# Moving a mixer's element work off GpSimd, and regrouping its small matmuls, in a two-layer RWKV trunk kernel

## The chip, the cores and the metric

The kernel runs on one core of one Trainium2 chip. The metric is device time of the whole program, in microseconds. TensorE (PE) multiplies, VectorE (DVE), ScalarE (ACT) and GpSimd (POOL) do element work, and SyncE (SP) issues most of the weight DMAs.

## The reference

Two layers of a decoder trunk run over 256 prompt tokens and 32 sample tokens (8 sequences of 4), all with the same weights. Each layer is a half-step FFN, a mixer, and a second half-step FFN:

```python
u = _modnorm(x, norm_g[l, 0], mod[:, :, 0], mod[:, :, 1])
x = x + 0.5 * mod[:, :, 2] * _swiglu(u, w_ffn_in[l, 0], w_ffn_out[l, 0])
u = _modnorm(x, norm_g[l, 1], mod[:, :, 3], mod[:, :, 4])
p = u @ w_in[l]
ya, S_T, sh = _rwkv7(p[..., :A_PROJ], ...)
yb, ph = _pool(p[..., A_PROJ:], pool_in[l], pos, w_pool[l], pool_scale[l])
gates = sigmoid(u @ w_gate[l] + b_gate[l])
merged = gates[..., :D_MODEL] * (ya @ w_br_a[l]) + gates[..., D_MODEL:] * (yb @ w_br_b[l])
x = x + mod[:, :, 5] * (merged @ w_out[l])
# then the second FFN like the first
```

The branch `_rwkv7` mixes each projected row with the row of the token before (`xs = pa + (prev - pa) * mu`), forms r, k, v, a decay, a and a gate g, runs a recurrence over tokens on a 64x64 state for each of 8 heads, normalises the result per head, adds a bonus (the sum of r*k*r_k times v) and multiplies by g. The branch `_pool` takes running means over 2, 4, 8 and 16 tokens for four groups of 128 channels. D_MODEL is 1024, A_WIDTH and B_WIDTH are 512.

## The kernel before, in words

Activations lie channel-major: 128 channels on the partitions, NT = 288 tokens along the free axis. The big products run in fp32r with a correction: each strip of four 128x128 weight tiles comes by DMA (`raw`), ACT rounds it to `wh` (L224), DVE forms the remainder `wl` (L225), and `mm3` issues three matmuls for a tile (L250), chained in one fixed order on PE. Four strips can be split ahead. All other matmuls are ordinary fp32.

A layer's mixer first projects u by the 19 tiles of w_in and the gates ("ga") by eight tiles for each branch. The list MAIN says in which order these strips come. A generator runs through MAIN; the recurrence's small work is written as code that calls `fill()` between its pieces, and each `fill()` runs a planned number of strips or queued items. A queued item is followed by two strips (WEAVE = 2). So every small piece of PE work stands between strips of big matmuls, and a pool strip's result is used by `pool_out` one "ga" strip after it.

Preparation makes four sets of 64-column blocks: A, B (`bb`), K and R, from xk, xr, aa (the in-context rate), ep and en (running decays). AR holds A and R, BK holds B and K. `scores(e, i, q)` multiplies four 64-row blocks of one row half e into one PSUM bank (L892), and DVE masks it out of PSUM into MM (L894). Four banks (`pswk`) serve these and all other small products. From MM a 15-step triangular inverse runs on DVE (L933 to L936), and its merges go back to PE (L1158, L1167). Then a loop over four chunks of 64 tokens carries the state (L1255, L1268). While it runs, the bonus of each pair of heads is spread by a matmul (L806) and the gate is made (L1113, L1114), each as a queued item of its own; `outputs`, group norms and the sample group's pieces follow in the same queue.

GpSimd takes in the mixer: the sample columns' three operations of a norm's end (L488, L489, L492), part of the token shift (L659), the copies and window sums of the pools (L668, L675, L686, L687), most products of the preparation (L834 to L880), r*k for the bonus (L958), and R times the decay (L968). Names used below: `psmm` and `pswk` are PSUM banks, `dd` is the pool branch's input to its matmul (L693), `rkk` is r*k, `xn`, `uh`, `ul` are a norm's result and its two parts.

Of the kernel before, what the change touches and what calls it, by code (L numbers as in the profile page):

```python
# [21 lines left out]
ALU = mybir.AluOpType  # L22
# [165 lines left out]
class Kernel:  # L188
# [281 lines left out]
    def u(self, l, sub, k0=0, k1=KD):  # L470

        nc = self.nc
        e3 = nc.gpsimd if l + sub else nc.vector
# [135 lines left out]
    def mixer(self, l):  # L609
# [39 lines left out]
        def shifted(i, ps, dst, early=False):  # L649

            mu = self.par(l, "mu", i)
            S.activation(out=dst, in_=ps[:, :NT], func=AF.Copy, scale=mu1[:, i:i + 1])
            S.copy(sho[:, i, :], ps[:, TP - 1:NT:TS])
            V.scalar_tensor_tensor(out=dst[:, 1:TP], in0=ps[:, 0:TP - 1], scalar=mu, in1=dst[:, 1:TP],
                                   op0=ALU.mult, op1=ALU.add)
            d3, p3 = self.smp(dst[:, TP:]), self.smp(ps[:, TP:NT])
            V.scalar_tensor_tensor(out=d3[:, :, 1:], in0=p3[:, :, 0:TS - 1], scalar=mu, in1=d3[:, :, 1:],
                                   op0=ALU.mult, op1=ALU.add)
            (V if early else G).tensor_tensor(out=d3[:, :, 0], in0=d3[:, :, 0], in1=shs[:, i, :], op=ALU.add)  # L659

        def pooled(g, ps):
# [6 lines left out]
            G.tensor_copy(pxs[:, :, 0:HIST], po[:, 1:, :])  # L668
# [17 lines left out]
            G.tensor_copy(po[:, 0, :], px[:, TP:TP + HIST])  # L686
            G.tensor_copy(po[:, 1:, :], pxs[:, :, TS:])  # L687
# [26 lines left out]
        def project_pre(m, ps):  # L714
            p = p0[:, m % KD, :]
            c = self.scaled(ps, p, V if m < 5 else G)
# [13 lines left out]
        def main_ops():  # L730

            for n, (name, m) in enumerate(MAIN):
# [101 lines left out]
        G.tensor_copy(gam[:, :, 0:NCH], ep[:, :, CH - 1:TP:CH])  # L834
        G.tensor_copy(gam[:, :, NCH:], ep[:, :, TP + TS - 1:NT:TS])
# [16 lines left out]

        for j in range(HP):
            S.activation(out=A[:, j], in_=chunks(xk[:, j, :]), func=AF.Copy, scale=self.par(l, "k_k", j))
        k_k = self.par(l, "k_k").unsqueeze(2)
        G.tensor_tensor(out=ARs[:, :, 0, :], in0=xk[:, :, TP:], in1=k_k.to_broadcast([P, HP, NS]), op=ALU.mult)
        G.tensor_tensor(out=bb[:, :, TP:], in0=ARs[:, :, 0, :], in1=aa[:, :, TP:], op=ALU.mult)
# [14 lines left out]
        for j in range(HP):  # L872
# [4 lines left out]
            with tc.issue_after(b_en.ins):  # L877
                G.tensor_tensor(out=R[:, j], in0=chunks(xr[:, j, :]), in1=chunks(ep[:, j, :]), op=ALU.mult)
        G.tensor_tensor(out=BKs[:, :, 1, :], in0=xk[:, :, TP:], in1=en[:, :, TP:], op=ALU.mult)
        G.tensor_tensor(out=ARs[:, :, 1, :], in0=xr[:, :, TP:], in1=ep[:, :, TP:], op=ALU.mult)  # L880
# [7 lines left out]
        def scores(e, i, q):  # L888
            ps = self.ps_wk()
            r = halves[e]  # L890
            for hp in range(HP):
                T.matmul(ps[:, 128 * hp:128 * hp + 128], BK[r, hp, i, 2 * q:2 * q + 2, :].rearrange("p x t -> p (x t)"),  # L892
                         AR[r, hp, 2 * i + q].rearrange("p x t -> p (x t)"), start=True, stop=True)
            V.tensor_tensor(out=MM[:, 2 * e + i, :, q].rearrange("p h x t -> p h (x t)"),  # L894
                            in0=ps.rearrange("p (h y) -> p h y", h=HP), in1=maskp, op=ALU.mult)
# [15 lines left out]
        for i in range(2):  # L911
            for q in range(2):
                for e in range(2):
                    scores(e, i, q)
# [40 lines left out]
        def rkk(j):  # L955

            t = tj("rkk")
            G.tensor_tensor(out=t, in0=xr[:, j, :], in1=xk[:, j, :], op=ALU.mult)  # L958
            return t

        def bonus():
# [5 lines left out]
            for c in range(1, NCH):  # L967
                G.tensor_tensor(out=R[:, :, c], in0=R[:, :, c], in1=gam[:, :, c - 1:c].to_broadcast([P, HP, CH]),  # L968
                                op=ALU.mult)
# [134 lines left out]
        def out_gate(j):  # L1104

            if j == 0:
# [378 lines left out]
```

## Time and profile before

| what | value |
|---|---|
| runs | 1456.34, 1459.24 and 1464.87 us, median 1459.24 |
| the profiled execution's own time | 1455.73 us |
| its span | 1453.9 us |
| PE / DVE / ACT / POOL busy | 1408.2 / 938.7 / 724.7 / 200.4 us |
| the two mixers | about 264 to 500 us and 978 to 1213 us |

PE is busy nearly all the time, so the profile is read from PE's idle gaps and from its small matmuls, then from the engine that ended each gap. The second mixer repeats the first some 713.7 us later with the same waits, so most rows are shown of the first alone. A row of a timeline gives the start, the duration and the instruction; consecutive starts on PE are what a matmul costs, since its recorded durations overlap.

### The profile page before, as it was taken

How to read it: one execution, taken by the hardware profiler on the slowest of the kernel's cores; microseconds unless marked ns; L12 is line 12 of the kernel's file. 1: busy time of each engine (PE TensorE's matmuls, PEld its weight loads, DVE VectorE, ACT ScalarE, POOL GpSimd, SP SyncE). 2: the span in 40 equal slices, each digit the busy share in tenths (PEclk: the TensorE clock that was granted, in tenths of full speed). 3: DMA queues.
4: the chain of work that ended last, by engine and by line, in shares of the span. 5: the costliest groups of instructions: out<-in, count | busy, mean ns of one | idle time of the engine just before them, and what ended most of it. 6: DMA issues, size and time to landing. Idle time of an engine off the chain costs nothing.

```text
span 1453.9 us, 30079 instructions
## 1 busy us (share of the span) xinstructions
PE 1408.2 (97%) x11872; PEld 1301.8 (90%) x11872; DVE 938.7 (65%) x1996; ACT 724.7 (50%) x1457; POOL 200.4 (14%) x294
## 2 busy tenths in 40 slices
PE   6999999998999999999999999999989999999997
PEld 5989999987778999899999999998877799999997
DVE  4645556898656885555667555669966678755554
ACT  4544444674534665444445445448553356645532
POOL 0000011163113010000211000122522110100012
PEclk9999999999999999999999999999999999999999
DMA  8888764443324666787657644553333257445552
GB/s 358 315 280 308 301 241 146 150 131 107 100 77 162 254 248 229 273 305 268 244 215 257 238 155 163 167 169 120 111 93 119 99 176 274 160 146 167 167 163 103
DMA packets 72382, 281.93 MB, mean 194 GB/s; under 512 B 9584, under 2 KB 11504, under 8 KB 62896
## 3 DMA queue, kind: packets, MB, share of 16 engines
q1 hardware_dynamic: 66384, 272.24, 53.0%
q10 hardware_dynamic: 5856, 7.77, 1.7%
q8 instruction: 93, 1.52, 0.4%
q14 instruction: 49, 0.40, 0.1%
HBM read 275.74 MB, written 4.23 MB: 193 GB/s over the span
## 4 chain that ended last, share of the span: by engine, by line
PE 85%; DVE 9%; issue 2%; ACT 1%; POOL 1%; DMA 1%; POOLq 0%; DVEq 0%; ACTq 0%
PE psmm L250 43%; PE pswk L250 30%; PE psmd L314 4%; DVE wl L225 3%; DVE ul L483 1%; DVE xn L480 1%; PE pswk L1134 1%; PE pswk L392 1%; PE pswk L902 0%; PE pswk L1036 0%; DVE g L936 0%; DMA s<-in_wkv 0%; PE pswk L1255 0%; DVE sh L933 0%; DMA cc<-in_c 0%
## 5 line engine op out<-in xcount | busy, mean ns | idle before, releaser
L225 DVE TENSOR_TENSOR wl<-raw,wh 128x512 fp32r<-128x512 f32 x732 | 522.2, 716 | 365.6 <-ACT wh L224 357.2
L224 ACT CAST wh<-raw 128x512 fp32r<-128x512 f32 x732 | 452.5, 620 | 564.8 <-PE psmm L250 296.2
L250 PE MATMUL psmm<-uh,wh 128*128 128x288 f32 x1072 | 324.2, 302 | 2.3 <-ACT uh L491 2.3
L250 PE MATMUL psmm<-uh,wl 128*128 128x288 f32 x1072 | 318.1, 297 | 4.0 <-DVE wl L225 4.0
L250 PE MATMUL psmm<-ul,wh 128*128 128x288 f32 x1072 | 318.1, 297 | 0.6 <-DVE ul L492 0.3
L250 PEld LDWEIGHTS psmm<-uh,wh 128*128 128x128 f32 x1072 | 202.6, 189 | 23.3 <-issue 11.9
L250 PEld LDWEIGHTS psmm<-uh,wl 128*128 128x128 f32 x1072 | 202.6, 189 | 8.1 <-DVE wl L225 5.2
L250 PEld LDWEIGHTS psmm<-ul,wh 128*128 128x128 f32 x1072 | 202.7, 189 | 3.1 <-issue 1.2
L250 PE MATMUL pswk<-ul,wh 128*128 128x288 f32 x608 | 179.6, 295 | 0.0
L250 PE MATMUL pswk<-uh,wl 128*128 128x288 f32 x608 | 179.5, 295 | 0.0
L250 PE MATMUL pswk<-uh,wh 128*128 128x288 f32 x608 | 179.5, 295 | 0.0
L377 POOL TENSOR_TENSOR sq<-x 128x288 f32<-128x288 f32 x28 | 19.8, 706 | 770.6 <-DVE x L519 770.6
L250 PEld LDWEIGHTS pswk<-uh,wh 128*128 128x128 f32 x608 | 114.6, 188 | 5.4 <-issue 4.2
L250 PEld LDWEIGHTS pswk<-ul,wh 128*128 128x128 f32 x608 | 114.6, 188 | 0.0
L250 PEld LDWEIGHTS pswk<-uh,wl 128*128 128x128 f32 x608 | 114.5, 188 | 0.0
L250 PE MATMUL pswk<-hl,wh 128*128 128x288 f32 x352 | 103.8, 295 | 0.0
L250 PE MATMUL psmm<-hl,wh 128*128 128x288 f32 x352 | 103.8, 295 | 0.0
L250 PE MATMUL psmm<-hh,wl 128*128 128x288 f32 x352 | 103.8, 295 | 0.0
L250 PE MATMUL pswk<-hh,wl 128*128 128x288 f32 x352 | 103.7, 295 | 0.0
L250 PE MATMUL psmm<-hh,wh 128*128 128x288 f32 x352 | 103.7, 295 | 0.0
L250 PE MATMUL pswk<-hh,wh 128*128 128x288 f32 x352 | 103.2, 293 | 0.0
L314 PE MATMUL psmd<-modw,csilu 128*32 128x512 f32 (+2 forms) x832 | 69.7, 475 | 9.0 <-DMA modw<-in_wmod 9.0
(337 smaller groups left out, 2484.0 us busy)
## 6 DMA issues: line engine op xcount, KB each, us to landing
raw<-in_wflat SPq DMA_DIRECT2D x366, 512.0 KB, 3.4
modw<-in_wmod SPq DMA_DIRECT2D x72, 1024.0 KB, 7.1
s<-in_wkv ACTq DMA_DIRECT2D x16, 256.0 KB, 3.2
o_wkvs<-s SPq DMA_DIRECT2D x8, 256.0 KB, 2.6
x<-in_x SPq DMA_DIRECT2D x1, 1152.0 KB, 5.3
o_y<-yo SPq DMA_DIRECT2D x2, 288.0 KB, 2.5
o_y<-yo ACTq DMA_DIRECT2D x2, 288.0 KB, 2.6
o_pool<-po SPq DMA_DIRECT2D x8, 67.5 KB, 2.4
```

What stands on the lines that cost most here:

```text
L224: self.nc.scalar.copy(wh, src)
L225: self.nc.vector.tensor_tensor(out=wl, in0=src, in1=wh.bitcast(F32), op=ALU.subtract)
L250: self.last = self.nc.tensor.matmul(ps, w, x, start=start and n == 0, stop=stop and n == 2)
L314: mm = nc.tensor.matmul(self.mod_ps[32 * q:32 * q + 32, :size], self.csilu[:, k, :], w[:, kk, q, :], start=(k == 0), stop=(k == KD - 1))
L377: nc.gpsimd.tensor_tensor(out=t, in0=x, in1=x, op=ALU.mult)
L392: nc.tensor.matmul(ps[:, i:i + 1], s[:, o:o + P], self.cst("ones"), start=n + i == 0, stop=n == len(self.sums) - 1 and i == 2)
L480: nc.vector.scalar_tensor_tensor(out=t, in0=self.x[:, k, :TP], scalar=g1, in1=r[:, :TP], op0=ALU.mult, op1=ALU.mult)
L483: nc.vector.scalar_tensor_tensor(out=ul, in0=t, scalar=s[:, k, 0:1], in1=uh.bitcast(F32), op0=ALU.add, op1=ALU.subtract)
L1134: T.matmul(ps[halves[e], :], BKTs[halves[e], hp, :], uv[halves[e]].rearrange("p b v -> p (b v)"), start=True, stop=True)
```

## The change

All of the following is in the mixer, but the first point, which is in every norm:

- The three sample operations at a norm's end go from GpSimd to DVE (five calls of `u` in the program; the very first was on DVE already).
- The token shift takes two DVE instructions instead of three: one over 287 columns, and a strided one of 8 columns that writes each sample sequence's first token anew. The sample columns of the last projected tiles go to DVE too.
- The window sums of the pools go to DVE, their copies to ACT.
- Preparation goes to DVE, partly in larger instructions: R in one of 1024 columns, `bb` times en in one of 1152. The four ACT copies that made A are dropped; two-operand products with a scalar take their place.
- `scores(i, q)` does both row halves, alternating matmuls between two banks, and then evicts both.
- The bonus and the gate are queued for two pairs of heads at once. The gate's 32-row remainder lies four times, on four row quarters, so that two of them can use different rows.
- MAIN has two "ga" strips ahead of the pool strips, and `pool_out` follows its strip as before.

The square for the norms, the power of the group norms, two sample operations and the gated state (L1260) stay on GpSimd.

```diff
 MAIN = [("in", m) for m in range(5, 15)]
+MAIN += [("ga", KD), ("ga", KD + 1)]
 for _m in range(4):
-    MAIN += [("in", 15 + _m), ("ga", KD + _m)]
-MAIN += [("ga", KD + _m) for _m in range(4, KD)]
+    MAIN += [("in", 15 + _m), ("ga", KD + 2 + _m)]
+MAIN += [("ga", KD + 6), ("ga", KD + 7)]
...
-        e3 = nc.gpsimd if l + sub else nc.vector
+        e3 = nc.vector
...
-            V.scalar_tensor_tensor(out=dst[:, 1:TP], in0=ps[:, 0:TP - 1], scalar=mu, in1=dst[:, 1:TP],
+            V.scalar_tensor_tensor(out=dst[:, 1:], in0=ps[:, 0:NT - 1], scalar=mu, in1=dst[:, 1:], op0=ALU.mult,
+                                   op1=ALU.add)
+            V.scalar_tensor_tensor(out=dst[:, TP::TS], in0=ps[:, TP:NT:TS], scalar=mu1[:, i:i + 1], in1=shs[:, i, :],
                                    op0=ALU.mult, op1=ALU.add)
-            d3, p3 = self.smp(dst[:, TP:]), self.smp(ps[:, TP:NT])
-            V.scalar_tensor_tensor(out=d3[:, :, 1:], in0=p3[:, :, 0:TS - 1], scalar=mu, in1=d3[:, :, 1:],
-                                   op0=ALU.mult, op1=ALU.add)
-            (V if early else G).tensor_tensor(out=d3[:, :, 0], in0=d3[:, :, 0], in1=shs[:, i, :], op=ALU.add)
...
-            G.tensor_copy(pxs[:, :, 0:HIST], po[:, 1:, :])
+            S.copy(pxs[:, :, 0:HIST], po[:, 1:, :])
...
-                G.tensor_tensor(out=nx[:, lo:], in0=cur[:, lo:], in1=cur[:, lo - d:PEXT - d], op=ALU.add)
+                V.tensor_tensor(out=nx[:, lo:], in0=cur[:, lo:], in1=cur[:, lo - d:PEXT - d], op=ALU.add)
...
-            S.activation(out=A[:, j], in_=chunks(xk[:, j, :]), func=AF.Copy, scale=self.par(l, "k_k", j))
+            V.scalar_tensor_tensor(out=bb[:, j, :], in0=xk[:, j, :], scalar=self.par(l, "k_k", j), in1=aa[:, j, :],
+                                   op0=ALU.mult, op1=ALU.mult)
...
-            G.tensor_tensor(out=chunks(bb[:, j, :]), in0=A[:, j], in1=chunks(aa[:, j, :]), op=ALU.mult)
-            V.tensor_tensor(out=A[:, j, :, 1:], in0=A[:, j, :, 1:], in1=chunks(ep[:, j, :])[:, :, :-1], op=ALU.mult)
-            b_en = G.tensor_tensor(out=bb[:, j, :], in0=bb[:, j, :], in1=en[:, j, :], op=ALU.mult)
+            V.scalar_tensor_tensor(out=A[:, j, :, 1:], in0=chunks(xk[:, j, :])[:, :, 1:], scalar=self.par(l, "k_k", j),
+                                   in1=chunks(ep[:, j, :])[:, :, :-1], op0=ALU.mult, op1=ALU.mult)
...
+        V.tensor_tensor(out=bb, in0=bb, in1=en, op=ALU.mult)
...
-                G.tensor_tensor(out=R[:, j], in0=chunks(xr[:, j, :]), in1=chunks(ep[:, j, :]), op=ALU.mult)
+        V.tensor_tensor(out=R, in0=xr[:, :, :TP].rearrange("p h (c t) -> p h c t", c=NCH),
+                        in1=ep[:, :, :TP].rearrange("p h (c t) -> p h c t", c=NCH), op=ALU.mult)
...
+            pss = [self.ps_wk(), self.ps_wk()]
             for hp in range(HP):
+                for e, r in enumerate(halves):
+                    T.matmul(pss[e][:, 128 * hp:128 * hp + 128], ...
...
-            G.tensor_tensor(out=t, in0=xr[:, j, :], in1=xk[:, j, :], op=ALU.mult)
+            V.tensor_tensor(out=t, in0=xr[:, j, :], in1=xk[:, j, :], op=ALU.mult)
...
-        def spread_bonus(j):
-            V.tensor_tensor(out=xv[:, j, :], in0=xv[:, j, :], in1=head_spread(bsum, j), op=ALU.mult)
+        def spread_bonus(js):
+            for j, ps in [(j, head_spread(bsum, j)) for j in js]:
+                V.tensor_tensor(out=xv[:, j, :], in0=xv[:, j, :], in1=ps, op=ALU.mult)
...
+                T.matmul(ps[:, :NT], g2b[r, :], sgl[r, 1, :], start=False, stop=True)
...
-                add(*[lambda j=j: spread_bonus(j) for j in range(HP)], *[lambda j=j: out_gate(j) for j in range(HP)],
+                add(*[lambda js=js: spread_bonus(js) for js in ((0, 1), (2, 3))],
+                    *[lambda js=js: out_gate(js) for js in ((0, 1), (2, 3))],
```

DVE's instructions around the first layer's scores, before (L225 splits a weight strip, L894 evicts scores, L875 and L876 make K, L654 and L657 are the token shift of `sgl`):

```order
L876 TENSOR_TENSOR BK<-xk,en 128x2x128
L875 TENSOR_TENSOR xk<-xk,ka 128x288 x2
L876 TENSOR_TENSOR BK<-xk,en 128x2x128
L654 SCALAR_TENSOR_TENSOR sgl<-psmm,par_84,sgl 128x255
L657 SCALAR_TENSOR_TENSOR sgl<-psmm,par_84,sgl 128x8x3
L876 TENSOR_TENSOR BK<-xk,en 128x2x128
L225 TENSOR_TENSOR wl_4060<-raw_3800,wh_4059 128x512
L225 TENSOR_TENSOR wl_4082<-raw_3800,wh_4081 128x512
L225 TENSOR_TENSOR wl_4124<-raw_3840,wh_4123 128x512
L894 TENSOR_TENSOR MM<-pswk,consts 128x4x128
L654 SCALAR_TENSOR_TENSOR sgl<-psmm,par_84,sgl 128x255
L894 TENSOR_TENSOR MM<-pswk,consts 128x4x128
```

The same stretch of DVE in the changed kernel (L226 splits, L897 evicts, L873 to L878 make K, R and the sample blocks, L655 and L658 are the token shift):

```order
L873 TENSOR_TENSOR xk<-xk,ka 128x288 x2
L874 TENSOR_TENSOR BK<-xk,en 128x2x128 x2
L873 TENSOR_TENSOR xk<-xk,ka 128x288
L875 TENSOR_TENSOR AR<-xr,ep 128x16x64
L874 TENSOR_TENSOR BK<-xk,en 128x2x128
L877 TENSOR_TENSOR BKs<-xk,en 128x4x32
L878 TENSOR_TENSOR ARs<-xr,ep 128x4x32
L655 SCALAR_TENSOR_TENSOR sgl<-psmm,par_84,sgl 128x287
L226 TENSOR_TENSOR wl_4033<-raw_3778,wh_4032 128x512
L897 TENSOR_TENSOR MM<-pswk,consts 128x4x128 x2
L658 SCALAR_TENSOR_TENSOR sgl<-psmm,mu_3070,shs 128x8
L226 TENSOR_TENSOR wl_4055<-raw_3778,wh_4054 128x512
```

R now stands on DVE in front of the scores, and one strip's split stands between two pairs of evictions, where three stood in front of the first.

PE around the bonus and the gate in the first layer, before (L806 spreads the bonus, L1113 and L1114 make the gate; between two of these visits stand twelve L250):

```order
L250 MATMUL psmm<-ybh,wl_5151 128x288
L806 MATMUL pswk<-bsum,consts 128x288
L250 MATMUL psmm<-ybh,wh_5180 128x288
```

```order
L250 MATMUL psmm<-ybh,wl_5181 128x288
L1113 MATMUL pswk<-sgl,g2a 128x288
L1114 MATMUL pswk<-sgl,g2b 128x288
L250 MATMUL psmm<-ybh,wh_5210 128x288
```

PE at the gate in the changed kernel (L1117 and L1120 are the gate, twice in one visit; the bonus has L806 x2 in the same way):

```order
L251 MATMUL psmm<-ybh,wl_5142 128x288
L1117 MATMUL pswk<-sgl,g2a 128x288 x2
L1120 MATMUL pswk<-sgl,g2b 128x288 x2
L251 MATMUL psmm<-ybh,wh_5178 128x288
```

The same matmuls stand in half as many visits, each with the second of its pair right behind the first.

## Rows read from the trace of the kernel before

**Rows 1.** Page, parts 1, 4, 5: busy time; chain by engine; one group.
```profile
PE 1408.2 (97%) x11872; PEld 1301.8 (90%) x11872; DVE 938.7 (65%) x1996; ACT 724.7 (50%) x1457; POOL 200.4 (14%) x294
...
PE 85%; DVE 9%; issue 2%; ACT 1%; POOL 1%; DMA 1%; POOLq 0%; DVEq 0%; ACTq 0%
...
L225 DVE TENSOR_TENSOR wl<-raw,wh 128x512 fp32r<-128x512 f32 x732 | 522.2, 716 | 365.6 <-ACT wh L224 357.2
```

**Rows 2.** Waits of PE, 264 to 500 us (first layer's mixer): total, times, longest.
```profile
PE psmm L693 <- DVE dd L682: 2.4, 1, 2.4
PE psmm L250 <- DVE wl L225: 2.0, 2, 1.7
...
PE pswk L964 <- POOL rkk L958: 1.0, 1, 1.0
PE pswk L892 <- DVE MM L894: 0.9, 1, 0.9
```

**Rows 3.** Timeline of PE, 321 to 333 us: start, duration, instruction [idle before it].
```profile
322.90 3.19 PE L892 MATMUL pswk<-AR,BK 64*128 64x128 f32 x32
327.00 4.09 PE L892 MATMUL pswk<-AR,BK 64*128 64x128 f32 x32 [0.91 <-DVE MM L894]
331.02 0.69 PE L964 MATMUL pswk<-rkk,rks 128*32 128x288 f32 x6
```

**Rows 4.** Timeline of DVE in the same stretch.
```profile
323.60 2.75 DVE L225 TENSOR_TENSOR wl<-raw,wh 128x512 fp32r<-128x512 f32 x3
...
329.20 2.47 DVE L894 TENSOR_TENSOR MM<-pswk,consts 128x512 f32<-128x512 f32 x4
```

**Rows 5.** Windows: length, busy time of PE, PEld, DVE, ACT, POOL, granted clock, DMA.
```profile
322.00:356.00 34.00, 29.69 (x216) 26.70 (x215) 31.93 (x104) 18.23 (x37) 13.58 (x22) 0.95 0.37 118
351.57:354.98 3.41, 3.41 (x14) 3.12 (x14) 2.47 (x10) 0.50 (x1) 0.29 (x1) 0.50 0.59 191
1041.06:1047.89 6.83, 6.83 (x36) 4.86 (x35) 6.19 (x13) 4.19 (x9) 3.08 (x5) 0.50 0.24 78
```

**Rows 6.** Timeline of PE, 404 to 425 us: a bonus visit, then a gate visit.
```profile
413.04 0.29 PE L250 MATMUL psmm<-uh,wl 128*128 128x288 f32 x1
413.27 0.75 PE L806 MATMUL pswk<-bsum,consts 32*128 32x288 f32 x2
413.94 0.40 PE L250 MATMUL psmm<-ybh,wh 128*128 128x288 f32 x1
...
419.30 0.65 PE L1113 MATMUL pswk<-sgl,g2a 128*128 128x288 f32 x2
419.88 0.75 PE L1114 MATMUL pswk<-sgl,g2b 32*128 32x288 f32 x2
420.55 0.40 PE L250 MATMUL psmm<-ybh,wh 128*128 128x288 f32 x1
```

**Rows 7.** Timeline of PE, 309.5 to 311 us: four row quarters spread together.
```profile
309.75 0.77 PE L806 MATMUL pswk<-rn,consts 32*128 32x288 f32 x8
```

**Rows 8.** Timeline of DVE, 270 to 273 us: part of a u() call.
```profile
270.94 1.86 DVE L480 SCALAR_TENSOR_TENSOR xn<-x,mod,rb 128x256 f32<-128x256 f32 x2
272.72 0.47 DVE L483 SCALAR_TENSOR_TENSOR ul<-xn,mod,uh 128x256 fp32r<-128x256 f32 x1
```

**Rows 9.** Groups of DVE by form, 264 to 400 us: count, busy time, mean ns.
```profile
L225 DVE TENSOR_TENSOR wl<-raw,wh 128x512 fp32r<-128x512 f32 x50 | 37.7, 762 | 10.5 <-ACT wh L224 10.4
...
L875 DVE TENSOR_TENSOR xk<-xk,ka 128x288 f32<-128x288 f32 x4 | 2.9, 738 | 0.0
...
L657 DVE SCALAR_TENSOR_TENSOR xv<-psmm,par,xv 128x24 f32<-128x24 f32 x4 | 0.9, 230 | 0.0
L462 DVE TENSOR_TENSOR p<-psmm,rb 128x288 f32<-128x288 f32 x4 | 1.8, 448 | 0.0
```

**Rows 10.** Groups of POOL, 264 to 400 us.
```profile
L675 POOL TENSOR_TENSOR pw<-pw 128x420 f32<-128x420 f32 (+2 forms) x6 | 5.9, 985 | 0.2
```

**Rows 11.** Waits of POOL, 264 to 500 us.
```profile
POOL px L668 <- DMA po<-in_poolh: 2.9, 2, 1.7
```

More of the change, by code (lines that the diff above doesn't have):

```diff
@@ L715, in project_pre @@
             p = p0[:, m % KD, :]
-            c = self.scaled(ps, p, V if m < 5 else G)
+            c = self.scaled(ps, p, V)
             V.tensor_scalar(p[:, :TP], p[:, :TP], c, None, op0=ALU.add)
@@ L886, in mixer, with scores @@
         MU = MM.rearrange("p g h q x t -> p (g h) q x t")
-        def scores(e, i, q):
-            ps = self.ps_wk()
-            r = halves[e]
+        def scores(i, q):
+            pss = [self.ps_wk(), self.ps_wk()]
             for hp in range(HP):
[L892 to L895, printed above, removed]
+                for e, r in enumerate(halves):
+                    T.matmul(pss[e][:, 128 * hp:128 * hp + 128],
+                             BK[r, hp, i, 2 * q:2 * q + 2, :].rearrange("p x t -> p (x t)"),
+                             AR[r, hp, 2 * i + q].rearrange("p x t -> p (x t)"), start=True, stop=True)
+            for e in range(2):
+                V.tensor_tensor(out=MM[:, 2 * e + i, :, q].rearrange("p h x t -> p h (x t)"),
+                                in0=pss[e].rearrange("p (h y) -> p h y", h=HP), in1=maskp, op=ALU.mult)
         def token_major(src, t=None):
@@ L912, in mixer @@
             for q in range(2):
-                for e in range(2):
-                    scores(e, i, q)
+                scores(i, q)
         m0, m1 = self.cst("halves")[:, 0:1], self.cst("halves")[:, 1:2]
@@ L965, in bonus @@
             S.copy(bsum, ps[:, :NT])
-            for c in range(1, NCH):
-                G.tensor_tensor(out=R[:, :, c], in0=R[:, :, c], in1=gam[:, :, c - 1:c].to_broadcast([P, HP, CH]),
-                                op=ALU.mult)
+            V.tensor_tensor(out=R[:, :, 1:], in0=R[:, :, 1:],
+                            in1=gam[:, :, 0:NCH - 1].unsqueeze(3).to_broadcast([P, HP, NCH - 1, CH]), op=ALU.mult)
         out = []
@@ L1111, in out_gate @@
             gw, (g2a, g2b) = out[1:]
-            ps = self.ps_wk()
-            T.matmul(ps[:, :NT], g2a[:, 128 * j:128 * j + 128], sgl[:, 0, :], start=True, stop=False)
-            T.matmul(ps[:, :NT], g2b[:, 128 * j:128 * j + 128], sgl[0:32, 1, :], start=False, stop=True)
-            S.activation(out=gw[:, j, :], in_=ps[:, :NT], func=AF.Copy, scale=self.par(l, "ln_w", j))
-            V.scalar_tensor_tensor(out=xv[:, j, :], in0=xv[:, j, :], scalar=self.par(l, "ln_b", j), in1=ps[:, :NT],
-                                   op0=ALU.add, op1=ALU.mult)
+            pss = [self.ps_wk() for _ in js]
+            for j, ps in zip(js, pss):
+                T.matmul(ps[:, :NT], g2a[:, 128 * j:128 * j + 128], sgl[:, 0, :], start=True, stop=False)
+            for j, ps in zip(js, pss):
+                r = quarter[j]
+                T.matmul(ps[:, :NT], g2b[r, :], sgl[r, 1, :], start=False, stop=True)
+            for j, ps in zip(js, pss):
+                S.activation(out=gw[:, j, :], in_=ps[:, :NT], func=AF.Copy, scale=self.par(l, "ln_w", j))
+                V.scalar_tensor_tensor(out=xv[:, j, :], in0=xv[:, j, :], scalar=self.par(l, "ln_b", j),
+                                       in1=ps[:, :NT], op0=ALU.add, op1=ALU.mult)
         def gated(t, ps, js=slice(0, HP)):
@@ L1411, in pack @@
     win[:, :, NPA * P:] = d["w_in"][:, :, A_PROJ:]
+    last = slice((NPA - 1) * P, A_PROJ)
+    win[:, :, A_PROJ:NPA * P] = np.tile(win[:, :, last], 3)
     src = {"fi": lambda l, f_: d["w_ffn_in"][l, f_], "fo": lambda l, f_: d["w_ffn_out"][l, f_],
@@ L1435, in pack @@
         for n, (off, w) in POFF.items():
-            par[l, :, off:off + w] = colmajor(d[names[n]][l], w)
+            a = d[names[n]][l]
+            par[l, :, off:off + w] = colmajor(np.concatenate([a] + 3 * [a[last]]) if n == "mu" else a, w)
     o["params"] = par
@@ L1444, in pack @@
     sh[:, :, :A_PROJ] = d["state_shift"][:, :, 0]
+    sh[:, :, A_PROJ:] = np.tile(sh[:, :, last], 3)
     o["shift"] = sh.reshape(DEPTH, NB, NPA, P).transpose(0, 3, 2, 1)
```

40 lines of the change are left out of this document (19 added, 21 removed).

## The prediction

> **What bounds the kernel now.** First the page's busy shares and its chain [rows 1]: PE is busy 97% of the span and holds 85% of the chain, DVE 9%, POOL 1%. The time is PE's work plus the gaps in it, and an instruction taken from POOL is worth nothing by itself. POOL's 200.4 us matter only where PE waits behind POOL, or where POOL delays DVE. Second, PE's waits in one mixer [rows 2]: the longest is L693 for `dd` (2.4 us), then `wl` splits (2.0), `rkk` from POOL (1.0) and a score eviction (0.9). Third, the place where they are thickest, the windows [rows 5]: from 322 to 356 us DVE is busy 31.93 of 34.00 us, so here DVE sets the pace and PE follows. The two windows below it show a granted clock of 0.50, the lower level of 1.2 GHz: one of 3.41 us right after PE's wait at L693, and in the second layer one of 6.83 us around its scores. At half clock their work took 1.7 and 3.4 us more than at 2.4 GHz, if it was PE that was the limit there. Everywhere else I take PE's own work as the time.
>
> The sum is made against the profiled execution's 1455.7 us, which is 3.5 us under the median of 1459.24; the difference found is then taken from the median.
>
> **The change, part by part.**
>
> *Bonus and gate in pairs.* These stand in the chunk loop, between strips of big products, where PE has no idle time shown [rows 6], so PE work removed is time removed. A bonus visit runs from 413.27 to 413.94, 0.67 us; with the matmul before it stretched (0.23 us from 413.04) it is 0.9 at most. A gate visit takes 0.58 for the full-height product and 0.67 for the 32-row one. Do two row quarters run together? Four of them took 0.77 us in the same instruction where one took 0.75 [rows 6, 7]. So a pair of bonuses costs one visit, and a pair of gates 2 x 0.58 + 0.67 = 1.83 in place of 2.50. Each of the four pairs in a layer thus saves 0.67, 2.7 a layer; with the visit's entry (up to 0.23) 3.6. Both layers: 5.4 to 7.2. I take **-6**. What could cancel it: the queue has four items fewer, so eight strips no longer stand among them but later. If the loop's DVE steps lose that cover, PE waits; that is the loss below.
>
> *From the norm to the end of the scores.* Here DVE decides. What is added on DVE, by the layer: three small operations of `u` (1.3, at 0.45 each as a 288-column product out of PSUM has it [rows 9]); `bb` four times (2.0); `bb` times en, 1152 columns, and R, 1024 columns (by the 288-column row 1.8 and 1.6 as an upper bound, since the fixed part is paid once; 1.3 and 1.2 with the 512-column split [rows 9] as the slope's guide); the sample blocks and A's first column, seven instructions of at most 128 columns at about 0.2 (1.5); three sample corrections (0.6). Sum 7.9. What is removed: the middle instruction of 15 shifts at 0.23 each [rows 9], 3.5, against ten first-token ones of about 0.17 that come from POOL and 32 columns more in each long one: net -1.2. So DVE has some **+6.7** to do before the scores end, in this layer.
>
> What it gets back is speed. Two L480 took 1.86 us while POOL worked on `xs`, and L483 of the same size right behind them 0.47 [rows 8]. The 50 splits of this stretch average 762 ns [rows 9], those of the whole program, these included, 716 [rows 1], and L875 takes 738 where a 288-column product out of PSUM takes 448. From the excess [rows 8, 9]: splits 50 x 0.05 = 2.3 at least, L480 1.0 or more, L875 1.2, and the other products of the preparation about 2: 6 to 7 us in 264 to 400 us, some 5 before the scores' end. The Trainium skill (SBUF — State Buffer, "Who interferes with whom") says that a VectorE instruction with two SBUF inputs contends with a GpSimd one that reads SBUF, and one with a single SBUF input does not; the 448 ns of the PSUM form against 738 agree. By that rule all 7 us come back, not the 5 I take, and the sum below would be 2 us a layer better.
>
> So before the scores DVE is about 1.7 us later in a layer (6.7 less 5), or 0.3 earlier with all 7 back. The scores themselves gain. Before, from 322.90 to 331.02 us, 8.12 us [rows 3]: the first eviction stands behind three splits of 2.75 us [rows 4], and PE, out of its four banks, waits. After, one split stands ahead of the first pair of evictions and one between pairs. An eviction costs 2.47 / 4 = 0.62 [rows 4], a split a little more. From the first score: two banks filled at about 1.0, evictions 1 and 2 until 2.6, a split and a small shift 0.8, evictions 3 and 4 until 4.6; the last two banks are filled by 5.6. That is **-2.5**. R, in one instruction, stands before the first score, where each head pair had its own before; it is inside the +6.7. Net of the stage: -0.8 (1.7 later) to -2.8 (0.3 earlier) a layer; I take the middle, **-2**, -4 for both. Bounds: nothing returned, +4.2 a layer; all returned and waits for `wl` gone, -4.5.
>
> *From the scores to the inverse's first matmul.* Gone: the wait of 2.4 us for `dd` [rows 2], whose window sums stood on POOL at 985 ns each [rows 10], the 1.0 for `rkk` from POOL [rows 2], and, if the wait goes, the clock dip after it. New: DVE does `rkk` (4 x 0.45), R times decay (768 columns, about 0.9) and the first window sums (420 columns, about 0.6 each) inside the same stretch as the 15-step inverse, 4.5 us, of which slowed steps return perhaps 2. Behind a wait of DVE for a pool strip's copy by ACT stand the inverse's steps, and PE's L1158 stands behind those. PE's work in that stretch is about as long as DVE's chain, so a part of the gain is eaten at that matmul. Gains 2.4 + 1.0 + 1.7 = 5.1, losses 2.5: about **-2.5** a layer, -5 for both. Bounds +2 and -5 a layer. The second layer's dip (3.4 us) is in the bounds of the total and not in the sum.
>
> *Losses.* ACT takes the history copy, which on POOL waited 2.9 us for its DMA in one mixer [rows 11]; behind it on ACT now stand weight rounds `wh`, and DVE's `wl` after those. With several strips split ahead I take 0.5 a layer; 2.9 if there is no slack. In the chunk loop fewer strips lie between the state's product and its use, where the copy of `UV` by ACT and DVE is then exposed: about two matmul visits, 1.0 a layer. Sum **+3** for both. `u` in the FFNs: 1.3 us of DVE each, against a slowing of about 1 that goes [rows 8]: nothing.
>
> Sum: -6 - 4 - 5 + 3 = **-12**, so 1443.7 for an execution like the profiled one and **1447** against the median.
>
> **The rivals.**
>
> *DVE becomes the bound (slower).* Where DVE is busy 31.93 of 34 us, every microsecond added there is PE's time if the slowing doesn't come back. Price: +6.7 and +4.5 a layer is +22; scores -5, pairs -6, losses +3, no gain at `dd`: +14, 1473. With a third returned it is about +8, 1467, and this is its centre. For it: the window's load. Against it: POOL's slowing of DVE is plain [rows 8, 9], and 10.5 us of idle DVE ahead of the splits, nearly all of it waiting for `wh` [rows 9], show slack in parts of the stretch. It decides if more than half of the 11 us a layer stays.
>
> *Only the pairs pay (the change does otherwise no more than move the waits).* Stage gains and losses cancel: the last score waits for R, `dd` waits for DVE's own queue in place of POOL's, L1158 comes at the same time. -6 + 3 = -3, with 3 us either way: 1453 to 1459.
>
> *All returns.* By the contention [rows 8, 9] in full, and with both clock dips gone (1.7 more in stage two, 3.4 in the second layer): -6 - 9 - 8 - 3.4 + 3 = -23, 1436.
>
> **How the numbers follow.** Forecast 0.50 (1440 to 1452), only the pairs 0.22, DVE the bound 0.16, all returns 0.12. What a measurement can tell from no change is about 0.5%, 7.3 us: faster below 1451.9, slower above 1466.5. Faster: nearly all of the forecast (0.48), all of the last rival, and 0.01 of the pairs' case, 0.61. Slower: most of DVE's case, 0.12. Same 0.27. The range leaves out half of the last rival and half of DVE's case: 1436 to 1466; the forecast's own is 1440 to 1452.
>
> **What would show it.** Right: in the loop after 404 us two bonus matmuls in one visit of about 0.7 us, gate visits of 1.8; the scores' stage under 6.5 us, with evictions in twos; no wait of L693 for a POOL tile; DVE's splits in the mixer at or under the 716 ns of the whole program; no stretch at clock 0.50 in the two mixers. Wrong: PE waits longer for `wl` or the first score before 331 us than the 2.0 and 0.9 of before; a wait at the inverse's first matmul of several us; ACT idle behind the history's DMA, with `wl` late next. The forecast fails if the time from the norm to the scores' end grows, or if the eight strips taken from the loop turn up as idle PE there.

## The result

The changed kernel takes 1441.34 us (median of 4 runs, 1439.83 to 1442.12) against 1458.87 for the kernel before: a ratio of 0.9866, interval 0.9844 to 0.9889, so 17.5 us faster. 1447 was forecast, with 1436 to 1466 as the range. The profiled execution took 1440.62 us, its span is 1438.8.

### The profile page after: what moved, and what is told of

Its sections match the earlier page's. It is cut to its first block, busy times and chain, and to the rows that moved or that the text cites. A ratio compares the mean times of both kernels' runs of the same rounds, so it can differ in the third digit from the quotient of the medians.

```text
span 1438.8 us, 29985 instructions
## 1 busy us (share of the span) xinstructions
PE 1395.2 (97%) x11872; PEld 1292.8 (90%) x11872; DVE 945.0 (66%) x2061; ACT 725.9 (50%) x1477; POOL 110.8 (8%) x155
## 4 chain that ended last, share of the span: by engine, by line
PE 87%; DVE 6%; DMA 2%; issue 2%; ACT 2%; POOL 1%; POOLq 0%; DVEq 0%; ACTq 0%
PE psmm L251 44%; PE pswk L251 31%; PE psmd L315 4%; DVE wl L226 2%; DMA s<-in_wkv 1%; PE pswk L905 1%; PE pswk L1037 1%; PE pswk L393 1%; ACT wh L225 1%; DVE MM L897 1%; DMA o_wkvs<-s 0%; DVE ul L484 0%; DVE xn L481 0%; PE pswk L1262 0%; DMA cc<-in_c 0%
## 5 line engine op out<-in xcount | busy, mean ns | idle before, releaser
L226 DVE TENSOR_TENSOR wl<-raw,wh 128x512 fp32r<-128x512 f32 x732 | 513.7, 704 | 352.3 <-ACT wh L225 341.2
L225 ACT CAST wh<-raw 128x512 fp32r<-128x512 f32 x732 | 452.6, 620 | 563.9 <-PE psmm L251 290.3
```

The lines of the kernel that those rows point to most:

```text
L225: self.nc.scalar.copy(wh, src)
L226: self.nc.vector.tensor_tensor(out=wl, in0=src, in1=wh.bitcast(F32), op=ALU.subtract)
```

## The profile after

Busy time of the changed kernel, and the group of the splits, as in [rows 1]:

```profile
PE 1395.2 (97%) x11872; PEld 1292.8 (90%) x11872; DVE 945.0 (66%) x2061; ACT 725.9 (50%) x1477; POOL 110.8 (8%) x155
...
PE 87%; DVE 6%; DMA 2%; issue 2%; ACT 2%; POOL 1%; POOLq 0%; DVEq 0%; ACTq 0%
...
L226 DVE TENSOR_TENSOR wl<-raw,wh 128x512 fp32r<-128x512 f32 x732 | 513.7, 704 | 352.3 <-ACT wh L225 341.2
```

GpSimd's busy time fell from 200.4 to 110.8 us and DVE's rose by only 6.3, although all of the preparation went there: the splits alone gave back 8.5 us (716 to 704 ns each). DVE's part of the chain went from 9% to 6%.

Waits of PE in the first layer's mixer, as in [rows 2]:

```profile
PE psmm L251 <- DVE wl L226: 2.9, 2, 1.6
PE pswk L893 <- DVE AR L875: 1.6, 1, 1.6
PE pswk L1037 <- DMA s<-in_wkv: 1.6, 1, 1.6
PE pswk L801 <- ACT xla L705: 1.3, 1, 1.3
PE pswk L1165 <- DVE dd L681: 1.1, 1, 1.1
PE pswk L966 <- DVE rkk L960: 0.9, 2, 0.6
```

The 2.4 us for `dd` at L693 are gone. But the list is not shorter: new are the first score's wait for R (L893 for AR), the inverse's first matmul (L1165), and longer ones for the sample state `s` and for `wl`. These are PE's and DVE's timelines around the scores, as in [rows 3] and [rows 4]:

```profile
321.88 2.06 PE L893 MATMUL pswk<-AR,BK 64*128 64x128 f32 x32 [1.62 <-DVE AR L875]
324.16 1.75 PE L893 MATMUL pswk<-AR,BK 64*128 64x128 f32 x16 [0.22 <-DVE MM L897]
326.09 1.75 PE L893 MATMUL pswk<-AR,BK 64*128 64x128 f32 x16 [0.18 <-DVE MM L897]
```

```profile
320.52 1.22 DVE L875 TENSOR_TENSOR AR<-xr,ep 128x1024 f32<-128x1024 f32 x1
...
322.82 0.68 DVE L226 TENSOR_TENSOR wl<-raw,wh 128x512 fp32r<-128x512 f32 x1
323.42 1.28 DVE L897 TENSOR_TENSOR MM<-pswk,consts 128x512 f32<-128x512 f32 x2
...
324.75 0.68 DVE L226 TENSOR_TENSOR wl<-raw,wh 128x512 fp32r<-128x512 f32 x1
325.35 1.28 DVE L897 TENSOR_TENSOR MM<-pswk,consts 128x512 f32<-128x512 f32 x2
```

From the first to the last pass of a score it is now 5.7 us (in the kernel before 7.9, from 322.90 to 330.82). PE waits 0.2 us before each later pair of banks and no longer 0.9 at once. In front of the first score stands R in one instruction of 1.22 us, for which PE waits 1.6.

The same stretch as in [rows 5] and the place of the old clock dip:

```profile
322.00:356.00 34.00, 30.63 (x334) 26.48 (x336) 32.74 (x112) 18.76 (x41) 1.19 (x4) 1.00 0.37 115
351.57:354.98 3.41, 2.49 (x19) 2.26 (x18) 3.34 (x12) 2.69 (x8) 0.00 (x0) 1.00 0.75 208
```

The granted clock is 1.00 in both. In the kernel before it was 0.50 in the second. The mean over the span rose from 0.993 to 0.998.

Where the time went, by the start of the same instruction in both timelines of PE (us):

| start of | before | after | after less before |
|---|---|---|---|
| layer 1: mixer's norm (L392, after L393) | 264.01 | 263.01 | -1.0 |
| first L801 of the mixer | 283.07 | 282.93 | -0.1 |
| first score | 322.90 | 321.88 | -1.0 |
| last score pass | 330.82 | 327.57 | -3.3 |
| inverse's first matmul | 357.15 | 355.15 | -2.0 |
| first product of the branch's output | 473.30 | 467.68 | -5.6 |
| layer 2: mixer's norm | 975.84 | 968.71 | -7.1 |
| first L801 of the mixer | 994.89 | 988.43 | -6.5 |
| first score | 1035.74 | 1027.54 | -8.2 |
| last score pass | 1044.45 | 1033.22 | -11.2 |
| inverse's first matmul | 1069.70 | 1060.92 | -8.8 |
| first product of the branch's output | 1187.11 | 1172.61 | -14.5 |
| end of span | 1453.94 | 1438.83 | -15.1 |

Between the last score and the inverse's first matmul there are now 142 big matmuls in place of 123, moved there by the order of the strips. At 0.132 us each that is 2.5 us, so the work-corrected change of that stretch is -1.3 and -0.1 us. The next stretch has 432 in place of 453, and its corrected change is -0.8 and -2.9. From the norm to the last score pass, where the forecast had -2 a layer, it is -2.3 and -4.1. The three FFN stretches behind the first mixer (from the norm that opens each to the next norm) became 0.7, 0.8 and 0.7 us shorter. They are so in the trace of every kernel with the moved work, and unchanged within 0.02 us in all the others.

The first 1.0 us stands ahead of the first mixer, where the change does nothing. In the thirteen traces that first mixer's norm starts between 262.5 and 265.2 us, so this 1.0 us is not counted as a gain below. By these rows the second mixer starts 711.8 us behind the first.

A bonus and a gate visit in the loop, as in [rows 6]:

```profile
404.32 0.75 PE L806 MATMUL pswk<-bsum,consts 32*128 32x288 f32 x4
...
409.17 1.13 PE L1117 MATMUL pswk<-sgl,g2a 128*128 128x288 f32 x4
410.23 0.76 PE L1120 MATMUL pswk<-sgl,g2b 32*128 32x288 f32 x4
410.91 0.40 PE L251 MATMUL psmm<-ybh,wh 128*128 128x288 f32 x1
```

Two bonuses take 0.75 us, as one did. A pair of gates takes 1.74 (409.17 to 410.91), where one took 1.25.

## The experiments

The interval in brackets is that of the ratio to the kernel before. Differences in us are between medians; the kernel before, run again beside each group of kernels, had medians of 1459.4 to 1460.1 us. The first four kernels have one part of the change alone, the next four all but that part.

**Pairs alone.** Only `spread_bonus(js)` and `out_gate(js)` with their data.

```diff
+                add(*[lambda js=js: spread_bonus(js) for js in ((0, 1), (2, 3))],
+                    *[lambda js=js: out_gate(js) for js in ((0, 1), (2, 3))],
```

> The kernel before with only the bonus and the gate queued in pairs of heads (and the data laid out for it). Theory A, the pairs are worth their matmuls (about 0.67 us for each of four visits saved in a layer), less a little that shows up as new waits: -4 to -6 us against before, all of it between the inverse's first matmul and the last strips of the mixer. Rival, the eight strips that no longer stand among the queued items were cover for the chunk loop and the sample group's pieces: -2 us or less, with new PE waits behind the state loads or the state copies. In the changed kernel that stretch became only 0.8 and 2.9 us shorter, which speaks for the rival.

Measured: 1457.3 us, ratio 0.9966 [0.9944, 0.9988], with runs from 1448.2 to 1460.6. The median, -2.5 us, lies near the rival's -2, but the interval takes in theory A's -4 to -6 as well, and the spread says more: the runs with mean clock 0.993 and 0.994 took 1448 us and those with 0.987 and 0.988 took 1459 to 1461. In the profiled run, the clock windows of this kernel show where (columns as in [rows 5]):

```profile
351.30:354.40 3.10, 3.10 (x11) 2.81 (x12) 2.58 (x10) 0.50 (x1) 0.04 (x1) 0.50 0.51 157
1074.80:1092.00 17.20, 17.20 (x268) 14.93 (x267) 4.40 (x9) 7.98 (x15) 1.51 (x3) 0.51 0.06 18
```

A stretch of 17.2 us at half clock follows a PE wait of 2.4 us at the inverse's merges in the second layer. The first layer's stretch from the last score to the branch's output became 2.7 us shorter, as theory A has it. So the matmuls are saved; that the clock took them back in most runs is read from the runs' mean clocks, since only one run has a trace.

**Scores alone.** Only `scores(i, q)`.

```diff
-                for e in range(2):
-                    scores(e, i, q)
+                scores(i, q)
```

> The kernel before with only the scores changed: both row halves alternate between two banks, then both are evicted. Theory A: the stage from the first to the last score goes from 7.9 to about 5.7 us, and in the second layer, where it ran partly at clock 0.50, from 8.7 to 5.7; PE keeps it: -4 to -6 us in all. Rival, DVE sets the pace there and the time returns at the next wl or at the inverse's first matmul: -1 us or less.

Measured: 1460.54 us, ratio 1.0001 [0.9985, 1.0016]. The stage did not shrink. The timelines of PE and DVE of this kernel:

```profile
321.32 2.30 PE L893 MATMUL pswk<-AR,BK 64*128 64x128 f32 x32
325.95 4.38 PE L893 MATMUL pswk<-AR,BK 64*128 64x128 f32 x32 [2.33 <-DVE MM L897]
```

```profile
322.01 2.75 DVE L225 TENSOR_TENSOR wl<-raw,wh 128x512 fp32r<-128x512 f32 x3
...
325.22 1.27 DVE L897 TENSOR_TENSOR MM<-pswk,consts 128x512 f32<-128x512 f32 x2
```

The three splits of 2.75 us still stand in front of the first eviction, and PE waits 2.3 us at once, more than the 0.9 of before. The clock is 0.50 from 326.7 to 330.1 us, right behind that wait. Theory A falls; the rival, that the time comes back later, isn't it either: nothing was gained in the first place.

**Moved work alone.** Everything that leaves GpSimd, and the two-step shift; pairs, scores and order as before.

```diff
-        e3 = nc.gpsimd if l + sub else nc.vector
+        e3 = nc.vector
...
+        V.tensor_tensor(out=R, in0=xr[:, :, :TP].rearrange("p h (c t) -> p h c t", c=NCH),
```

> The kernel before with only the work moved off GpSimd and the shorter token shift (no pairs, scores and order of strips as before). Theory A, GpSimd slowed DVE by about as much as the moved work adds there: the 50 splits from 264 to 400 us fall from 762 to under 695 ns on average, the norm's end is 0.3 us faster in each of five calls, dd's wait goes from 2.4 to about 1: -3 to -7 us. Rival, DVE has more to do and PE waits for it: +2 us or more, with a longer time from the norm to the first score.

Measured: 1454.52 us, ratio 0.9967 [0.9951, 0.9983]: -5, inside theory A's range. And it is this kernel, with its scores by row halves, that has the short stage. Its PE timeline:

```profile
323.75 5.59 PE L891 MATMUL pswk<-AR,BK 64*128 64x128 f32 x64 [1.62 <-DVE AR L874]
```

All 64 passes run in 5.59 us; from the start of the first to that of the last it is 5.3, by which measure the changed kernel has 5.7. On DVE, R now stands ahead of the first score, no split stands between it and the first eviction, and the later splits stand one at a time between evictions. The 50 splits of 264 to 400 us average 684 ns, as theory A has it. Its `dd` wait is a miss: 2.6 us in place of about 1, behind the old order of strips, and the granted clock is 0.66 on average in 340 to 345 us and in 1035 to 1040. What the stage gave, the next stretch took back: from the last score to the branch's output it is 4.0 and 2.2 us longer than before. In this trace the two mixers together are no shorter, and what lasts is the 2.2 us of the three FFNs; the profiled execution of the kernel before, to which it is held here, lay 4 us under that kernel's median.

**Order alone.** Only MAIN, and `pool_out`'s index.

```diff
+MAIN += [("ga", KD), ("ga", KD + 1)]
```

> The kernel before with only the order of strips changed (two ga strips ahead of the pool strips). Theory A: the window sums on GpSimd get two strips more cover, so PE's wait of 2.4 us for dd and the clock dip after it shrink in the first layer, the inverse's first matmul stays bound by DVE: -1 to -4 us. Rival, the order matters only together with the moved work: within 1 us.

Measured: 1458.91 us, ratio 0.9983 [0.9965, 1.0002], which excludes neither the rival's "within 1 us" nor theory A's -1 to -4. In the trace, from the last score to the inverse it is 3.5 and 2.9 us better after correction for the moved matmuls, as expected, but the next stretch gives back 1.5 and 3.7.

**All but the pairs.**

> The changed kernel with the bonus and the gate queued one head pair at a time again. Theory, the pairs are worth their matmuls (5.4 to 7.2 us) less the waits behind the sample state's loads that now stand closer together (2.0 and 1.7 us before the last strips in the first layer): 3 to 6 us slower than the changed kernel, 1444 to 1448, and those two waits gone. Rival, their cover was worth as much: within 1.5 us of the changed kernel.

Measured: 1446.13 us (1445.16 to 1446.26), ratio 0.9886 [0.9864, 0.9908]. So the pairs are worth 4.8 us in the whole by the medians, and 3.1 us in the two mixers by the traces. The waits for `wl` at the mixer's end are gone, as expected: PE's waits in the first mixer don't list `wl` any more.

**All but the alternating scores.**

> The changed kernel with the scores by row halves again. Theory after the single parts were run: it was the moved work that shortened the scores' stage (2.6 us there, against 0.8 us longer with the alternation alone), since a later preparation puts fewer splits between the evictions; so the alternation is worth 1 us or less a layer: 0 to 2 us slower than the changed kernel. Rival, as forecast: the alternation is worth 2.5 us a layer, 4 to 6 us slower.

Measured: 1440.36 us, ratio 0.9851 [0.9823, 0.9880]: 1.0 us faster than the changed kernel, which the intervals don't tell from no difference. Row halves take 5.59 us from PE here too, as with the moved work alone. The alternation has no gain that these runs show.

**All but the order.**

> The changed kernel with the strips in the old order. Theory: the two ga strips ahead of the pool strips cover dd's wait; alone they made the stretch from the scores to the inverse 3.5 and 2.9 us shorter, the moved work alone made it 2.0 and 2.2 us longer: 4 to 8 us slower than the changed kernel, with a wait at L693 or at the inverse's first matmul of over 2 us and clock 0.50 behind it. Rival, the wait only moves to the inverse's first matmul: within 2 us.

Measured: 1452.0 us, ratio 0.9933 [0.9904, 0.9962]: 10.7 slower than the changed kernel, more than was expected, and not where it was expected: the wait for `dd` is 1.1 us, not over 2. Windows of this kernel at two PE waits and just after each (columns as above):

```profile
383.00:386.00 3.00, 0.98 (x7) 0.63 (x8) 2.33 (x10) 1.02 (x2) 0.00 (x0) 1.00 0.42 168
386.50:390.00 3.50, 3.50 (x32) 2.63 (x31) 2.98 (x9) 0.00 (x0) 0.61 (x1) 0.52 0.23 75
452.00:454.30 2.30, 0.57 (x5) 0.42 (x4) 1.76 (x3) 2.30 (x6) 0.99 (x1) 1.00 0.00 0
454.50:458.00 3.50, 3.50 (x18) 3.50 (x17) 3.09 (x6) 0.01 (x1) 0.24 (x1) 0.53 0.67 213
```

PE is busy 0.98 of 3.00 us, and then 0.52 is granted for 3.5 us; busy 0.57 of 2.30 us, and then 0.53. Two more such dips stand in the second layer. In the changed kernel a wait stands at the first of these places too (1.6 us at L1037), and no dip follows it.

**All but the moved work.**

> The changed kernel with the moved work back on GpSimd (pairs, alternating scores and the new order stay). Theory, the moved work is worth more than its own waits, since it also keeps PE from the pauses after which the clock fell: 6 to 10 us slower than the changed kernel, mean clock 0.994 or lower. Rival, pairs and order alone bring most of it: under 4 us slower.

Measured: 1456.83 us, ratio 0.9974 [0.9956, 0.9991], mean clock 0.986 to 0.991: 15.5 slower than the changed kernel, beyond the theory's 6 to 10. Without the moved work the pairs, the order and the scores together bring 0.3%.

**GpSimd kept reading.**

```diff
+        junk = tl([P, P], "junk")
+        G.tensor_tensor(out=junk, in0=xla[:, 0:P], in1=self.cst("scan")[:, 0:P], op=ALU.mult)
+        for _ in range(35):
+            G.tensor_tensor(out=junk, in0=junk, in1=self.cst("scan")[:, 0:P], op=ALU.mult)
```

> The changed kernel with 36 products of 128x128 on GpSimd at the start of the preparation in each layer, whose result nobody uses: about 18 us of GpSimd reading two operands from SBUF while DVE prepares. Theory, GpSimd's reading slows DVE's instructions with two SBUF operands, and DVE sets the pace there: DVE's products beside it take 1.4 to 2 times as long, the first score comes 2 to 4 us later in each layer: 4 to 8 us slower than the changed kernel. Rival, the moved work pays by what PE and ACT no longer wait for on GpSimd, not by DVE's speed: within 1.5 us.

Measured: 1447.79 us, ratio 0.9916 [0.9891, 0.9941]: 6.5 slower than the changed kernel. Counted from the norm, the first score comes 3.2 and 2.6 us later. GpSimd's added work in the first layer (its first product starts at 284.31 us):

```profile
284.81 24.49 POOL L854 TENSOR_TENSOR junk<-junk,consts 128x128 f32<-128x128 f32 x35
```

DVE's groups of this kernel and then of the changed one, 264 to 330 us: the token shift from an SBUF tile (`xk`), `bb`, the same shift from PSUM (`xr`), and a maximum with a constant on one SBUF tensor (`rn`):

```profile
L655 DVE SCALAR_TENSOR_TENSOR xk<-p,par,xk 128x287 f32<-128x287 f32 x4 | 2.7, 689 | 0.0
L857 DVE SCALAR_TENSOR_TENSOR bb<-xk,par,aa 128x288 f32<-128x288 f32 x4 | 2.4, 643 | 0.0
...
L655 DVE SCALAR_TENSOR_TENSOR xr<-psmm,par,xr 128x287 f32<-128x287 f32 x3 | 1.5, 503 | 0.0
...
L826 DVE TENSOR_SCALAR rn<-rn 128x288 f32<-128x288 f32 x1 | 0.5, 516 | 0.0
```

```profile
L655 DVE SCALAR_TENSOR_TENSOR xk<-p,par,xk 128x287 f32<-128x287 f32 x4 | 2.0, 518 | 0.3 <-ACT xk L653 0.3
...
L853 DVE SCALAR_TENSOR_TENSOR bb<-xk,par,aa 128x288 f32<-128x288 f32 x4 | 1.9, 515 | 0.0
...
L655 DVE SCALAR_TENSOR_TENSOR xr<-psmm,par,xr 128x287 f32<-128x287 f32 x3 | 1.5, 514 | 0.0
...
L826 DVE TENSOR_SCALAR rn<-rn 128x288 f32<-128x288 f32 x1 | 0.3, 306 | 0.0
```

In the first of the two kernels all these instructions start between 284.3 and 307.2 us, while GpSimd's products run. With two tensors from SBUF the shift of `xk` goes from 518 to 689 ns and `bb` from 515 to 643; the shift of `xr`, whose first operand is in PSUM, goes from 514 to 503. So theory A of the moved work holds: nobody used GpSimd's result here, and DVE was slower by its reading alone. The Trainium skill (SBUF — State Buffer, "Who interferes with whom") states that a VectorE instruction with two SBUF inputs contends with a GpSimd instruction that reads SBUF, and that one with at most one SBUF input, outside the 2-port perf modes, does not; the rows of `xk`, `bb` and `xr` agree, with a factor of 1.25 to 1.33. `rn` has one SBUF input and went from 306 to 516 ns, one instruction in each kernel; whether it ran in such a mode the trace doesn't tell.

**Two tiles for the last state loads.** Here and in the next kernel the scores are by row halves.

```diff
-            s0 = tl([P, NB, 64], "O0", "s0")
+            s0 = tl([P, NB, 64], ("O0", "en")[hp % 2], "s0")
```

> The changed kernel with the scores by row halves again, and with the sample state's last four loads on two tiles in turn in place of one. Theory: in the changed kernel ACT stands 4.4 and 3.7 us in front of a load that waits until the store from the same tile has ended, the weight rounds behind it come late, and PE waits 2.0 and 1.7 us for wl in the first layer, 1.3 and 1.2 in the second. With two tiles two of the four loads need no store's end soon: 3 to 5 us faster than the kernel with scores by row halves (1440.4), 1435 to 1438. Rival, the strips were late because DVE was: within 1 us of it.

Measured: 1440.6 us, ratio 0.9867 [0.9845, 0.9889], against 1440.36: nothing. One of the two waits for `wl` at the mixer's end is gone from the trace, which made that stretch 1.0 us shorter in each layer; PE's wait for the sample state at L1035, 2.0 us, stayed, and in the profiled run a clock dip follows it. A miss.

**The last state loads on GpSimd's queue.**

```diff
-            s0 = tl([P, NB, 64], "O0", "s0")
-            nc.scalar.dma_start(out=s0, in_=self.io["wkv"][l][:, hp])
...
+            s0 = tl([P, NB, 64], "O0", "s0")
+            nc.gpsimd.dma_start(out=s0, in_=self.io["wkv"][l][:, hp])
```

> The changed kernel with the scores by row halves again, and with the sample state's last four loads issued on GpSimd's queue, behind each piece's product there, in place of ACT's. ACT then waits for no store of the state. Theory: the weight rounds come in time, PE's waits for wl before the last strips of the mixer (2.0 and 1.7 us in the first layer of the changed kernel) go: 2 to 5 us faster than the kernel with scores by row halves (1440.4). Rival, after the two tiles brought nothing: these waits have another cause, or GpSimd's later products make PE wait instead, within 1 us or slower.

Measured: 1447.49 us, ratio 0.9916 [0.9891, 0.9942], 7 slower. DVE's timeline of this kernel at the two sums of the state, and then that of the changed kernel:

```profile
451.32 0.69 DVE L1141 TENSOR_TENSOR s<-s,pswk 128x512 f32<-128x512 f32 x1 [4.67 <-DMA s<-in_wkv]
...
462.54 0.69 DVE L1141 TENSOR_TENSOR s<-s,pswk 128x512 f32<-128x512 f32 x1 [5.56 <-DMA s<-in_wkv]
```

```profile
447.26 0.69 DVE L1143 TENSOR_TENSOR s<-s,pswk 128x512 f32<-128x512 f32 x1 [1.40 <-DMA s<-in_wkv]
...
456.97 0.69 DVE L1143 TENSOR_TENSOR s<-s,pswk 128x512 f32<-128x512 f32 x1 [2.67 <-DMA s<-in_wkv]
457.58 2.74 DVE L226 TENSOR_TENSOR wl<-raw,wh 128x512 fp32r<-128x512 f32 x3
```

DVE stands idle 4.7 and 5.6 us in front of the sum, waiting for the load, where it was 1.4 and 2.7; the splits queued behind are late, and PE waits for them. So the waits for `wl` come at least in part from DVE, which stands in its own order behind the load. What ACT's freedom is worth this kernel can't show, because its loads also took longer from issue to landing (last number, us), while GpSimd waited 9.3 us in the first layer for the stores before it issued them:

```profile
s<-in_wkv ACTq DMA_DIRECT2D x8, 256.0 KB, 2.5
s<-in_wkv POOLq DMA_DIRECT2D x8, 256.0 KB, 4.4
```

With the pairs, the sample's four pieces stand closer together, and one load after the other must wait for the store from the same tile.

## Why the prediction was right, and which steps were not

The sign and the range held, and the size to within half as much again: -12 forecast, -17.5 measured between medians and -15.1 in the two profiled executions, of which 1.0 stands ahead of the first mixer. The steps did worse than the sum. The norms' stretches and the FFNs gave 4.6 us more than forecast and the stretch to the inverse 3.6 less, so that the total came as near as it did is in part luck.

*Bonus and gate in pairs, -6.* The mechanism is right: visits of 0.75 and 1.74 us, and 4.8 us by the kernel without them. In the stretch behind the inverse's first matmul the change is -3.8 for both layers, against the -3 that -6 and the losses of +3 make. The loss of cover stood in another entry; what was lost is the wait for `wl` at the mixer's end, which the prediction saw as a copy of `UV` and which by the rows is mainly the sample state's sum on DVE.

*From the norm to the end of the scores, -4.* Measured -6.4 (2.3 and 4.1; in the second layer the scores of before ended in the clock dip). The first score was forecast 0.3 us earlier to 1.7 later, and, counted from the norm, is 0.0 and 1.1 earlier. One sign of being wrong came: PE waits 1.6 us in front of the first score, more than the 0.9 of before, but the stretch as a whole shrank. That GpSimd's silence gives DVE back about as much as it gets to do is thus right, and the kernel with GpSimd kept reading shows it by itself. The trace of before shows it too. These are DVE's splits and `xk` products beside GpSimd's products (306.56 to 315.05 us), and behind them:

```profile
306.80 2.52 DVE L225 TENSOR_TENSOR wl<-raw,wh 128x512 fp32r<-128x512 f32 x2
...
310.46 1.06 DVE L875 TENSOR_TENSOR xk<-xk,ka 128x288 f32<-128x288 f32 x1
...
318.45 0.68 DVE L225 TENSOR_TENSOR wl<-raw,wh 128x512 fp32r<-128x512 f32 x1
...
321.58 0.82 DVE L875 TENSOR_TENSOR xk<-xk,ka 128x288 f32<-128x288 f32 x2
```

The two splits beside GpSimd take 1.3 us each and the later one 0.68; an `xk` product takes 1.06 beside it and 0.45 behind, and the 738 ns that the prediction reads is the mean of both kinds (450 in the changed kernel). The prediction set these 738 ns against the 448 of a product out of PSUM; those products ran between 278 and 290 us, where GpSimd did next to nothing, so that comparison shows nothing of GpSimd's reading; the rows of `xr` above do.

The step that failed is the one on the scores, in its cause: "After, one split stands ahead of the first pair of evictions and one between pairs" gave the right length (5.6 forecast, 5.7 measured), and it counted this as a gain of the new scores. The order of DVE shown ahead of the prediction was that of the whole change. The kernel with the scores alone kept the three splits in front and gained nothing; the kernel with the moved work alone takes 5.3 by the same measure.

*From the scores to the inverse, -5.* Mis-sized: -1.4 for both layers with the moved strips taken out. The waits for `dd` and, for the most part, `rkk` went, as forecast. In their place came 1.1 and 1.2 us at the inverse's first matmul, 0.9 for `rkk` on DVE, and 0.7 at L693 for ACT, in each layer: DVE's own window sums stand inside the inverse's chain.

*Losses, +3.* The history copy cost little: ACT waits 2.3 us for its DMA in the first mixer, and no wait of PE is put down to it. PE's wait for the sample state at L1037 doubled (0.8 us before, 1.6 now), which was not among the losses named. `u` in the FFNs, entered at nothing, is mis-sized: the three FFN stretches gave 2.2 us, and only the kernels with the moved work have them.

*The clock.* The prediction kept the second layer's dip out of the sum and gave "both clock dips gone" a chance of 0.12. The trace of the changed kernel has neither. Its other three runs have no trace, but mean clocks of 0.997 and 0.998. In 31 runs of the kernel before the time goes with the mean clock, from about 1458 us at 0.993 to 1469.84 at 0.983, about 1 us for 0.001; 0.005 more is thus, as an estimate, some 5 of the 17.5 us.

The clock also bears on why the parts don't add up: alone the pairs, the scores, the order and the moved work bring 2.5, -0.8, 0.9 and 5.3 us by their medians, 7.9 in all, while taking them out of the whole costs 4.8, -1.0, 10.7 and 15.5. With a straight line of time against mean clock through each kernel's own runs, read at 0.992, they bring 7.6, -0.2, 1.1 and 3.1 us alone, 11.6 in all. From 0.992 to the changed kernel's 0.998 the line of the kernel before gives 6.4 us more, which makes 18.0. So a part alone leaves waits behind which the clock falls, and the runs' mean clocks account for about what is missing. This is an estimate from runs that differ by themselves; no run changed the clock alone.

One sum of the rivals is off by a little: with a third of DVE's +22 returned, its case comes to +7 and 1466, not +8; neither the range nor a chance hangs on it.

Not settled: why some waits of PE of 2 us are followed by a dip and others aren't. The order of strips is worth 0.9 us alone and 10.7 in the whole, and its dips stand far from the strips that it moves.

## What to carry to other kernels

Look at the granted clock right behind each wait of TensorE before pricing it: in these runs a wait of 1 to 4 us was often followed by 3 to 20 us at half clock. While such waits are left, parts tried one at a time can look worth less than they are in the whole. When GpSimd runs two-operand work beside a saturated VectorE, count what it takes from VectorE: moving it over can be nearly free. And an order of instructions taken from a whole change says what will stand where, but not which edit put it there; price each edit from an order of its own.

## What was not expected of the hardware

Every dip to 0.50 in the traces of these kernels began within about 2 us of the end of a PE pause of 0.9 to 3.8 us (from the end of one matmul to the end of the next), and lasted 3 to 20 us; the changed kernel's mixers have pauses of 1.7 to 2.2 us with no dip behind them. Two examples of such dips are in the windows of the kernel without the new order.

The same product of 288 columns on GpSimd in the kernel before, and on DVE in the changed one:

```profile
L958 POOL TENSOR_TENSOR rkk<-xr,xk 128x288 f32<-128x288 f32 x4 | 4.1, 1030 | 5.2 <-DVE xk L875 5.2
```

```profile
L960 DVE TENSOR_TENSOR rkk<-xr,xk 128x288 f32<-128x288 f32 x4 | 1.8, 455 | 0.0
```

1030 ns against 455. The 1030 is a mean of two kinds. Two of the four, from GpSimd's timeline of the kernel before:

```profile
315.79 0.81 POOL L958 TENSOR_TENSOR rkk<-xr,xk 128x288 f32<-128x288 f32 x1
...
324.56 1.24 POOL L958 TENSOR_TENSOR rkk<-xr,xk 128x288 f32<-128x288 f32 x1
```

Beside the first, DVE ran instructions with an operand in PSUM; beside the second, two splits with both tensors in SBUF, which took 0.94 and 1.28 us in place of 0.68. The other two took 1.28 and 0.79 us. So here the two engines slowed each other where both read two tensors from SBUF; where DVE didn't, GpSimd takes about 1.8 times what DVE takes for this product (0.81 to 0.455).
